# A two-layer decoder trunk: every compute engine in written order, one stream of weights, x transposed on the chip

## The chip, the core and the metric

The kernel runs on one core of a Trainium2 chip. Its engines are TensorE (PE: products and transposes), ScalarE (ACT), VectorE (DVE) and GpSimd (POOL); SyncE (SP) issues most transfers. Each engine works through its own list in order and waits at semaphores. The metric is the time of one execution in microseconds on the device.

## What is computed

Two pre-norm residual layers over 256 positions of width 1024, in float32. Layer 0 mixes with two parallel groups of eight heads: A, latent attention with low-rank q and kv and rotated parts, and B, dilated attention, written here as one table of biases. Layer 1 mixes with grouped-query attention over a window of 128 with a learned sink for each head. Each mixer is followed by a SwiGLU block of width 2816. From the reference, cut:

```python
h = x
for layer in range(DEPTH):                       # 2
    hn = _rmsnorm(h, attn_norm[layer])
    if layer % 2 == 0:
        mix = _even_mixer(hn, w_in, g_q, g_kv, w_uq, w_ukv, w_out, cos, sin, dil_slopes)
    else:
        mix = _odd_mixer(hn, w_qkv, sinks, w_out, swa_slopes)
    h = h + mix
    h = h + _swiglu(_rmsnorm(h, ffn_norm[layer]), w_gate_up[layer], w_down[layer])
return _rmsnorm(h, final_norm)
```

## The kernel before

**Products in three parts.** A float32 factor is split into hi, its value rounded to the engine's fp32r format, and lo, the rest. A product is then hi x hi, hi x lo and lo x hi, three matmuls into one PSUM tile (`mm3`, L116 to L126). A tile named `wh_x` is the hi copy of weight x, `wl_x` its rest, `raw_x` what arrived.

**Weights.** They arrive in units of up to 1 MB in a pool of three (`raw`), on SyncE's queue. Chunks of 128 x 512 are split: the hi copy on ScalarE (L93), the rest on VectorE or, for parts of b, wo0, qc and wo1, on GpSimd (`rest`, L73 to L78; L94). Seven pieces (two chunks each) fit in the pool of split weights. Names: c the joint low-rank projection, b the q, k, v of group B, uq and ukv the expansions of A, wo0 and wo1 the output projections, gu and dn the feed-forward blocks, kv and qc the projections of layer 1.

**The start.** x arrives twice: transposed (`xT`, eight row blocks, in five transfers), from which ScalarE and VectorE make the hi and lo parts with the gain (`xTh`, `xTl`), and plain (`h`), for norms and residuals. Then the products with c, the norms of c (`rstd_n`, `rstd_c`), the first products with b, transposes of c (`cT`), uq and ukv, and the rotation of q (`qA`).

**Attention.** Heads go in pairs: a0 to a3, b0 to b3 in layer 0, c0 to c7 in layer 1. A pair takes transposes of q and k (`T`), scores (`s`), on VectorE the minimum of the negated score with bias (`sn`, `nm`), on ScalarE the exponential with its sum (`e`, `sm`), the reciprocal (`rs`), on GpSimd the normalisation (L422), on TensorE the transposes of the weights (`pT`), their split into `pTh` (ScalarE) and `pTl` (VectorE), the values (`o`), and their split (`oT`). In layer 1 GpSimd writes the negated sink of each head into two columns of `sn` (L402). Iteration i runs the scores of pair i, the transposes of pair i + 1 and the values of pair i - 1, with other products between (`attention`, L479).

**Feed-forward.** For each of eleven groups of 256 columns: gate and up in one tile (`f0g`), Silu, product, transpose, and then the products with dn. The new h is formed in four quarters (`new_h`, L619): added (`h`), scaled by the gain (`hg`), transposed (`hT`) and split (`hTh`, `hTl`).

**Order.** TensorE's list is written by hand in the early part, the attentions and the end of each output projection; elsewhere, and on all other engines, a scheduler orders the work. Helpers hold several operations in one line, so rows name tiles.

## Time and profile before

| | |
|---|---|
| median of 3 runs | 590.8 us (589.92 to 591.53) |
| the profiled execution | 591.05 us |
| its span | 589.3 us |
| TensorE busy | 563.4 us, 96% |
| VectorE busy | 361.1 us, 61% |
| ScalarE busy | 335.9 us, 57% |
| GpSimd busy | 94.0 us, 16% |
| transferred | 101.57 MB, mean 172 GB/s |

A busy TensorE has matmuls in flight, each of which overlaps the next; the share says where none was in flight, not how fast they ran. Busy times of the other engines count their instructions alone.

### The profile page before, as it was taken

Reading aid. Unit: us, or ns where it says so; the run is one execution under the profiler, and the core shown is the slowest. Engines: PE = TensorE matmul, PEld = TensorE weight load, DVE = VectorE, ACT = ScalarE, POOL = GpSimd, SP = SyncE. Lnnn points to the kernel's source line nnn. Section 1 sums busy time; section 2 is a strip of 40 time slices with the busy share of each in tenths; the row PEclk is TensorE's granted clock in tenths of the full one; section 3 lists DMA queues with packets and bytes.
Section 4 is the critical chain, followed back from the end, with each engine's and each line's share of the span. In section 5 each row is a group of like instructions: output and inputs, shape, how many; then the busy total and the mean of one; then the engine's idle time right before and its main releaser. Section 6 shows DMA issues by size and latency. Waiting matters only on the chain.

```text
span 589.3 us, 7653 instructions
## 1 busy us (share of the span) xinstructions
PE 563.4 (96%) x2661; PEld 459.1 (78%) x2661; DVE 361.1 (61%) x742; ACT 335.9 (57%) x732; POOL 94.0 (16%) x157
## 2 busy tenths in 40 slices
PE   7798999899999999999999999999999999999995
PEld 5587787778888888888888777768888888888884
DVE  4578678786655565554559468777556556654524
ACT  5687788656545555544338787756555455454412
POOL 1169653110000000000001664300000000000000
PEclk9899999999999999999999999999999999999998
DMA  7777523336555555555546534226555565555301
GB/s 246 294 254 266 199 83 115 105 142 237 167 191 202 162 207 171 186 195 172 205 143 216 194 117 170 73 72 213 199 196 185 174 212 157 202 190 173 137 1 71
DMA packets 18183, 101.57 MB, mean 172 GB/s; under 512 B 2272, under 2 KB 3168, under 8 KB 7520
## 3 DMA queue, kind: packets, MB, share of 16 engines
q1 hardware_dynamic: 17712, 100.55, 49.5%
q10 hardware_dynamic: 432, 0.53, 0.2%
q8 instruction: 21, 0.34, 0.2%
q14 instruction: 18, 0.15, 0.1%
HBM read 100.02 MB, written 1.05 MB: 172 GB/s over the span
## 4 chain that ended last, share of the span: by engine, by line
PE 76%; ACT 8%; DVE 7%; DMA 3%; issue 2%; POOL 2%; SPq 0%; POOLq 0%; DVEq 0%; ACTq 0%
PE f0g L126 7%; PE f1g L126 7%; PE f1g L124 7%; PE f0g L124 7%; PE f1g L125 7%; PE f0g L125 7%; PE f0d L124 3%; PE f0d L125 3%; PE f0d L126 3%; PE f1d L124 3%; PE f1d L125 3%; PE f1d L126 3%; DMA h<-in_x_dram 2%; PE p L124 1%; DVE wl_gu L94 1%
## 5 line engine op out<-in xcount | busy, mean ns | idle before, releaser
L94 DVE TENSOR_TENSOR wl_gu<-raw_gu,wh_gu 128x512 fp32r<-128x512 f32 x176 | 116.4, 693 | 67.7 <-ACT wh_gu L93 66.1
L93 ACT CAST wh_gu<-raw_gu 128x512 fp32r<-128x512 f32 x176 | 102.2, 619 | 76.1 <-PE f0g L126 33.1
L94 DVE TENSOR_TENSOR wl_dn<-raw_dn,wh_dn 128x512 fp32r<-128x512 f32 x88 | 57.5, 689 | 54.8 <-ACT wh_dn L93 54.8
L93 ACT CAST wh_dn<-raw_dn 128x512 fp32r<-128x512 f32 x88 | 50.8, 619 | 61.6 <-PE f1d L126 23.3
L124 PE MATMUL f1g<-wh_gu,hTh_p 128*128 128x512 f32 x176 | 69.7, 396 | 0.0
L124 PE MATMUL f0g<-wh_gu,hTh_p 128*128 128x512 f32 x176 | 69.7, 396 | 0.0
L126 PE MATMUL f0g<-wh_gu,hTl_p 128*128 128x512 f32 x176 | 68.7, 390 | 0.7 <-DVE hTl_p L142 0.7
L126 PE MATMUL f1g<-wh_gu,hTl_p 128*128 128x512 f32 x176 | 68.7, 390 | 0.6 <-DVE hTl_p L142 0.6
L125 PE MATMUL f0g<-wl_gu,hTh_p 128*128 128x512 f32 x176 | 68.5, 389 | 0.0
L125 PE MATMUL f1g<-wl_gu,hTh_p 128*128 128x512 f32 x176 | 68.5, 389 | 0.0
L126 PEld LDWEIGHTS f0g<-wh_gu,hTl_p 128*128 128x128 f32 x176 | 33.0, 188 | 8.1 <-DVE hTl_p L142 1.1
L126 PEld LDWEIGHTS f1g<-wh_gu,hTl_p 128*128 128x128 f32 x176 | 33.0, 188 | 8.1 <-DVE hTl_p L142 1.1
L124 PEld LDWEIGHTS f0g<-wh_gu,hTh_p 128*128 128x128 f32 x176 | 33.1, 188 | 6.5 <-ACT hTh_p L141 0.2
L125 PEld LDWEIGHTS f0g<-wl_gu,hTh_p 128*128 128x128 f32 x176 | 33.1, 188 | 6.5
L125 PEld LDWEIGHTS f1g<-wl_gu,hTh_p 128*128 128x128 f32 x176 | 33.1, 188 | 6.4
L124 PEld LDWEIGHTS f1g<-wh_gu,hTh_p 128*128 128x128 f32 x176 | 33.1, 188 | 6.5
L124 PE MATMUL f0d<-wh_dn,f0fTh 128*128 128x512 f32 x88 | 34.5, 392 | 0.0
L124 PE MATMUL f1d<-wh_dn,f1fTh 128*128 128x512 f32 x88 | 34.3, 390 | 0.0
L126 PE MATMUL f0d<-wh_dn,f0fTl 128*128 128x512 f32 x88 | 34.3, 390 | 0.0
L126 PE MATMUL f1d<-wh_dn,f1fTl 128*128 128x512 f32 x88 | 34.2, 389 | 0.0
L125 PE MATMUL f1d<-wl_dn,f1fTh 128*128 128x512 f32 x88 | 34.2, 389 | 0.0
L125 PE MATMUL f0d<-wl_dn,f0fTh 128*128 128x512 f32 x88 | 34.2, 389 | 0.0
(299 smaller groups left out, 1134.9 us busy)
## 6 DMA issues: line engine op xcount, KB each, us to landing
raw_gu<-in_w_gu_dram SPq DMA_DIRECT2D x44, 1024.0 KB, 4.8
raw_dn<-in_w_dn_dram SPq DMA_DIRECT2D x22, 1024.0 KB, 4.8
raw_wo<-in_w_wo_dram SPq DMA_DIRECT2D x8, 1024.0 KB, 5.1
raw_b<-in_w_b_dram SPq DMA_DIRECT2D x4, 1024.0 KB, 5.1
raw_qc<-in_w_qc_dram SPq DMA_DIRECT2D x4, 1024.0 KB, 4.9
bias<-in_bias_dram SPq DMA_DIRECT2D x12, 256.0 KB, 3.9
raw_b<-in_w_b_dram SPq DMA_DIRECT2D x4, 512.0 KB, 10.0
gain<-in_gains_dram SPq DMA_DIRECT2D x4, 512.0 KB, 4.0
```

Of the source, the lines that this page charges most:

```text
L93: nc.scalar.copy(hi[:, a:e], part)
L94: rest(name, u).tensor_sub(lo[:, a:e], part, hi[:, a:e].bitcast(F32))
L124: nc.tensor.matmul(out, ah, wh, start=first, stop=False)
L125: nc.tensor.matmul(out, ah, wl, start=False, stop=False)
L126: nc.tensor.matmul(out, al, wh, start=False, stop=last)
```

## The change

The lists of TensorE, ScalarE, VectorE and GpSimd are now all as written in the program; SyncE's is still the scheduler's. The weights are one stream in a written order: c, two units of b, uq, ukv, the rest of b, wo0, gu0, dn0, kv, qc, wo1, gu1, dn1. A chunk is split after each 1024 columns of products (`settle`), up to eight chunks ahead of their use (`AHEAD`); a unit is loaded two units ahead. Outside the attentions ScalarE makes all hi copies and VectorE all rests. In the attentions ScalarE and VectorE take turns at the hi copies, GpSimd makes all rests, and the chunks are split at the end of an iteration. xT is not loaded any more: x arrives in eight pieces of 128 x 256, TensorE transposes it in sixteen transposes, and hi and lo are made from PSUM. Three products that only keep TensorE busy are added. The rotation of q is on VectorE for both halves (before: GpSimd for one). The squares of the feed-forward norms come after seven triples of products, Silu one triple later, the transposes of the new h 1500 columns after its sum (before 2000 or 2100). The attention is cut into pieces (minimum, exponential, normal, upper, lower) whose order is written.

```diff
--- before.py
+++ after.py
@@ -22,19 +22,8 @@
...
+    engines = mybir.EngineType
+    ctx.enter_context(
+        tc.manual_schedule(engines={engines.PE, engines.Activation, engines.DVE, engines.Pool}))
...
+    order = ["c", "b", "uq", "ukv", "b", "wo0", "gu0", "dn0", "kv", "qc", "wo1", "gu1", "dn1"]
+    early_b = 2
+    units = []
...
-    def rest(name, u):
-        if name not in POOLED or (name in ("b", "qc") and u < 3):
-            return nc.vector
-        pooled[0] += 1
-        return nc.vector if pooled[0] % 3 == 0 else nc.gpsimd
...
+    def emit_chunk():
+        i, name, p, base, a, e = chunks[state["emitted"]]
+        state["emitted"] += 1
+        while state["loaded"] <= min(i + 2, len(units) - 1):
+            load_next()
+        if (name, p) not in pieces:
...
+        if state["mode"] == "plain":
+            nc.scalar.copy(hi[:, a:e], part)
+            nc.vector.tensor_sub(lo[:, a:e], part, hi[:, a:e].bitcast(F32))
+        else:
+            state["turn"] += 1
+            if state["turn"] % 2:
                 nc.scalar.copy(hi[:, a:e], part)
-                rest(name, u).tensor_sub(lo[:, a:e], part, hi[:, a:e].bitcast(F32))
...
+            else:
+                nc.vector.tensor_copy(hi[:, a:e], part)
+            nc.gpsimd.tensor_sub(lo[:, a:e], part, hi[:, a:e].bitcast(F32))
...
+    AHEAD = 8
+    def pump(n):
+        for _ in range(n):
+            if state["emitted"] < len(chunks) and state["emitted"] - state["used"] < AHEAD:
+                emit_chunk()
...
+    def settle():
+        n = state["columns"] // 1024
+        state["columns"] -= 1024 * n
+        pump(n)
...
+        state["columns"] += out.shape[-1]
+        if state["auto"]:
+            settle()
+        for it in list(later):
...
+    def load_x(q):
+        for b in range(2):
+            nc.sync.dma_start(h[b][:, q * 256 : (q + 1) * 256], dr["x"][b * P : (b + 1) * P, q * 256 : (q + 1) * 256])
+    for q in range(3):
+        load_x(q)
+        load_next()
+    load_x(3)
...
+    state["auto"] = False
     for q in range(4):
-        xq = big.tile([P, 512], F32, tag="big", name=f"xT{q}")
+        pt = any_att(f"xT{q}")
+        for j in range(2):
+            for b in range(2):
+                nc.tensor.transpose(
+                    pt[:, (2 * j + b) * P : (2 * j + b + 1) * P],
+                    h[b][:, (2 * q + j) * P : (2 * q + j + 1) * P], ident)
         hi = tpool.tile([P, 512], F32R, tag="hTh", bufs=4, name=f"xTh{q}")
         lo = tpool.tile([P, 512], F32R, tag="hTl", bufs=4, name=f"xTl{q}")
...
                 hT[b][1][kt] = lo[:, j * S + b * P : j * S + (b + 1) * P]
+            emit_chunk()
         if q == 0:
-            load("c", 2, lambda: nc.sync.dma_start(xq[:, 0:256], dr["xT"][:, 0:256]))
-            nc.sync.dma_start(xq[:, 256:512], dr["xT"][:, 256:512])
-            part_weight("c", lambda: part_x(0))
+            keep_warm(3, False, True)
...
     mask = cpool.tile([P, S], F32, tag="mask", name="mask")
-    load("b")
-    load("uq")
-    load("ukv")
-    nc.sync.dma_start(rope, dr["rope"].rearrange("p (b t f) -> p b t f", b=2, t=3))
-    nc.sync.dma_start(mask, dr["mask"])
-    cT, kr, cgs = [], [], []
+    pump(2)
     ms0 = small.tile([P, 2], F32, tag="ss2", name="ss_n0")
-    for b in range(2):
-        mean_squares(h[b], 1.0 / 32.0, ms0[:, b : b + 1], f"n0{b}")
+    mean_squares(h[0], 1.0 / 32.0, ms0[:, 0:1], "n00")
+    pump(1)
+    mean_squares(h[1], 1.0 / 32.0, ms0[:, 1:2], "n01")
+    pump(1)
     rstd0 = rsqrt_eps(ms0, "n0")
...
+    def rotate(b, half):
+        r = qA[b][half]
+        x1, x2 = r[:, :, 64:80], r[:, :, 80:96]
+        cos, nsin, sin = (rope[:, b, i, :].rearrange("p (h f) -> p h f", f=16) for i in range(3))
+        tt = [work.tile([P, 4, 16], F32, tag="ropet", bufs=4, name=f"ropet{b}{half}{i}") for i in range(2)]
+        nc.vector.tensor_mul(tt[0], x2, nsin)
+        nc.vector.tensor_mul(tt[1], x1, sin)
+        nc.vector.tensor_mul(x1, x1, cos)
+        nc.vector.tensor_mul(x2, x2, cos)
+        nc.vector.tensor_add(x1, x1, tt[0])
+        nc.vector.tensor_add(x2, x2, tt[1])
+    for half in range(2):
+        for b in range(2):
...
-            eng = nc.gpsimd if half else nc.vector
...
+        def begin(self, i):
+            sn = work.tile([P, 386], F32, tag="sn", bufs=3, name=f"sn_{self.name}{i}")
+            nm = small.tile([P, 2], F32, tag="nm", name=f"nm_{self.name}{i}")
+            sm = small.tile([P, 2], F32, tag="sm", name=f"sm_{self.name}{i}")
+            if self.sinks[i] is not None:
+                nc.gpsimd.tensor_copy(sn[:, 128:130], self.sinks[i].to_broadcast([P, 2]))
+            self.st[i] = sn, nm, sm
         def scores(self):
...
+        def minimum(self, k):
+            b, i = self.order[k]
+            if self.st[i] is None:
+                self.begin(i)
+            sn, nm, sm = self.st[i]
             n, a, ba = ((128, 0, 128), (256, 130, 0))[b]
+            sink = self.sinks[i]
             nc.vector.tensor_tensor_reduce(
-                out=sn[:, a : a + n], in0=ps, in1=bias[:, ba:256], op0=ALU.add, op1=ALU.min,
+                out=sn[:, a : a + n], in0=self.ps[i][b], in1=self.bias(i)[:, ba:256], op0=ALU.add, op1=ALU.min,
...
+            if cur:
+                cur.minimum(0)
+            if done:
+                done.lower(1)
+            if cur:
+                cur.exp(0)
+                cur.minimum(1)
+                cur.exp(1)
+                cur.minimum(2)
+                cur.minimum(3)
+            other(i, 2 if many > 4 else 1)
+            rest = ahead[0]() if ahead else []
+            if last:
+                last.turn_p(0)
+            do(rest[:1])
+            other(i, 1)
+            rest2 = ahead[1]() if len(ahead) > 1 else []
+            if last:
+                last.turn_p(1)
+            do(rest[1:])
+            do(rest2)
+            if i + 1 < n:
+                pairs[i + 1].begin(0)
+            if cur:
+                cur.exp(2)
+                if not cur.split:
+                    cur.normal(0)
+                cur.exp(3)
+                if cur.split:
+                    cur.normal(0)
+                cur.normal(1)
+            other(i, many)
+            settle()
+            if last:
...
         gu = f"gu{layer}"
-        parts = {}
+        after(7 * 512, lambda: rs.extend(row_rstd(name)))
...
+            after(512, lambda ch=ch, pg=pg: gated(ch, pg))
```

The first place is SyncE's list in the start; raw_c is a unit of c, raw_b one of b, h the plain x. x2 marks two rows that read alike. Before:

```order
L65 DMA raw_c_2_135<-in_w_c_dram 128x832
L185 DMA xT2_132<-in_xT_dram 128x512
L65 DMA raw_c_3_151<-in_w_c_dram 128x832
L185 DMA xT3_148<-in_xT_dram 128x512
L196 DMA h0_214<-in_x_dram 128x1024
L196 DMA h1_215<-in_x_dram 128x1024
L65 DMA raw_b_0_218<-in_w_b_dram 128x1024 x2
L199 DMA gqkv_233<-in_gqkv_dram 128x384
L65 DMA raw_b_1_235<-in_w_b_dram 128x1024 x2
L65 DMA raw_b_2_252<-in_w_b_dram 128x2048
L65 DMA raw_uq_0_254<-in_w_uq_dram 128x1536
L65 DMA raw_ukv_0_256<-in_w_ukv_dram 128x1024
```

Now:

```order
L188 DMA h0_101<-in_x_dram 128x256
L188 DMA h1_102<-in_x_dram 128x256
L254 DMA gqkv_257<-in_gqkv_dram 128x384
L338 DMA rope_259<-in_rope_dram 128x384
L360 DMA mask_260<-in_mask_dram 128x256
L640 DMA bias0_926<-in_bias_dram 128x512
L640 DMA bias1_1037<-in_bias_dram 128x512
L640 DMA bias2_1132<-in_bias_dram 128x512
L702 DMA gain0_1418<-in_gains_dram 128x1024
L78 DMA raw_c_3_158<-in_w_c_dram 128x416 x2
L78 DMA raw_b_0_190<-in_w_b_dram 128x1024 x2
L78 DMA raw_b_1_222<-in_w_b_dram 128x1024 x2
```

The loads of rope, mask, bias and gain stood behind the units of b, and now stand ahead of the fourth unit of c.

The second place is GpSimd's list in attention 1, around pair c2; sn is the sink copy, e the normalisation, wl_wo1 the rests. Before:

```order
L94 TENSOR_TENSOR wl_wo1_1_1_3682<-raw_wo1_1_3673,wh_wo1_1_1_3681 128x512
L402 COPY sn_c21_3386<-nsink_2994 128x2
L422 TENSOR_SCALAR e_c10_3284<-e_c10_3284,rs_c10_3287 128x128
L422 TENSOR_SCALAR e_c10_3284<-e_c10_3284,rs_c10_3287 128x256
L402 COPY sn_c30_3467<-nsink_2994 128x2
L422 TENSOR_SCALAR e_c11_3290<-e_c11_3290,rs_c11_3293 128x128
L422 TENSOR_SCALAR e_c11_3290<-e_c11_3290,rs_c11_3293 128x256
L94 TENSOR_TENSOR wl_wo1_2_0_3850<-raw_wo1_2_3847,wh_wo1_2_0_3849 128x512
L94 TENSOR_TENSOR wl_wo1_2_1_3856<-raw_wo1_2_3847,wh_wo1_2_1_3855 128x512
L402 COPY sn_c31_3473<-nsink_2994 128x2
L422 TENSOR_SCALAR e_c20_3381<-e_c20_3381,rs_c20_3384 128x128
```

Now:

```order
L467 TENSOR_SCALAR e_c11_3330<-e_c11_3330,rs_c11_3372 128x128
L467 TENSOR_SCALAR e_c11_3330<-e_c11_3330,rs_c11_3372 128x256
L102 TENSOR_TENSOR wl_wo1_1_3383<-raw_wo1_0_3147,wh_wo1_1_3382 128x512 x2
L433 COPY sn_c21_3411<-nsink_3034 128x2
L433 COPY sn_c30_3453<-nsink_3034 128x2
L467 TENSOR_SCALAR e_c20_3409<-e_c20_3409,rs_c20_3459 128x128
L467 TENSOR_SCALAR e_c20_3409<-e_c20_3409,rs_c20_3459 128x256
L467 TENSOR_SCALAR e_c21_3416<-e_c21_3416,rs_c21_3463 128x128
L467 TENSOR_SCALAR e_c21_3416<-e_c21_3416,rs_c21_3463 128x256
L102 TENSOR_TENSOR wl_wo1_2_3478<-raw_wo1_1_3192,wh_wo1_2_3477 128x512 x2
```

The copy for c21 (second head of pair c2) stood ahead of the normalisations of pair c1 and stands now behind them and two rests of wo1.

The third place is VectorE's list where attention 0 ends and feed-forward 0 begins; h is the new sum, hg with its gain, hTl its rest. Before:

```order
L624 TENSOR_TENSOR hg_p010_1423<-h1_215,gain0_1380 128x512
L142 TENSOR_TENSOR hTl_p000_1434<-hT_p000_1428,hTh_p000_1433 128x512
L622 TENSOR_TENSOR h1_215<-p011_996,h1_215 128x512
L142 TENSOR_TENSOR hTl_p001_1480<-hT_p001_1474,hTh_p001_1479 128x512
L624 TENSOR_TENSOR hg_p011_1441<-h1_215,gain0_1380 128x512
L206 TENSOR_SCALAR ss_f01_1452<-ss_f01_1452 128x1
L94 TENSOR_TENSOR wl_gu0_2_1_1582<-raw_gu0_2_1573,wh_gu0_2_1_1581 128x512
L142 TENSOR_TENSOR hTl_p010_1492<-hT_p010_1486,hTh_p010_1491 128x512
L94 TENSOR_TENSOR wl_gu0_3_0_1623<-raw_gu0_3_1620,wh_gu0_3_0_1622 128x512
L142 TENSOR_TENSOR hTl_p011_1507<-hT_p011_1501,hTh_p011_1506 128x512
L94 TENSOR_TENSOR wl_gu0_3_0_1623<-raw_gu0_3_1620,wh_gu0_3_0_1622 128x512
L673 SCALAR_TENSOR_TENSOR f0f00_1565<-f0g00_1458,rstd_f00_1449,f0s00_1563 128x256
```

Now:

```order
L95 TENSOR_TENSOR wl_gu0_1_1453<-raw_gu0_0_1183,wh_gu0_1_1452 128x512
L708 TENSOR_TENSOR h1_102<-p010_1024,h1_102 128x512
L710 TENSOR_TENSOR hg_p010_1457<-h1_102,gain0_1418 128x512
L162 TENSOR_TENSOR hTl_p000_1468<-hT_p000_1462,hTh_p000_1467 128x512
L95 TENSOR_TENSOR wl_gu0_1_1453<-raw_gu0_0_1183,wh_gu0_1_1452 128x512
L162 TENSOR_TENSOR hTl_p001_1482<-hT_p001_1476,hTh_p001_1481 128x512
L708 TENSOR_TENSOR h1_102<-p011_1025,h1_102 128x512
L710 TENSOR_TENSOR hg_p011_1486<-h1_102,gain0_1418 128x512
L162 TENSOR_TENSOR hTl_p010_1501<-hT_p010_1495,hTh_p010_1500 128x512
L95 TENSOR_TENSOR wl_gu0_2_1510<-raw_gu0_1_1351,wh_gu0_2_1509 128x512
L162 TENSOR_TENSOR hTl_p011_1522<-hT_p011_1516,hTh_p011_1521 128x512
L95 TENSOR_TENSOR wl_gu0_2_1510<-raw_gu0_1_1351,wh_gu0_2_1509 128x512
```

A piece of gu0 is two chunks. Before, five pieces were split ahead of hTl_p000 and the sixth (wl_gu0_2_1: second of the third unit) stood beside it; now it is the second (wl_gu0_1), and the third stands behind the work on the last quarter of h.

## Rows read from the trace of the kernel before

**Rows 1.** The page, busy time, share of the span and instructions by engine.

```profile
PE 563.4 (96%) x2661; PEld 459.1 (78%) x2661; DVE 361.1 (61%) x742; ACT 335.9 (57%) x732; POOL 94.0 (16%) x157
```

**Rows 2.** Stretches: length, busy PE, PEld, DVE, ACT, POOL (x instructions), clock, DMA.

```profile
0.00:32.30 32.30, 24.50 (x98) 18.10 (x99) 15.10 (x35) 17.74 (x40) 4.33 (x13) 0.95 0.78 269
...
50.50:118.20 67.70, 63.62 (x339) 51.24 (x338) 48.57 (x147) 51.47 (x146) 32.80 (x47) 1.00 0.43 148
...
134.00:312.00 178.00, 178.00 (x813) 147.46 (x812) 102.72 (x168) 88.52 (x165) 2.13 (x4) 1.00 0.54 184
312.00:333.70 21.70, 20.46 (x119) 17.21 (x118) 14.12 (x24) 16.60 (x36) 8.40 (x7) 1.00 0.68 232
333.70:389.50 55.80, 52.87 (x276) 41.78 (x275) 40.79 (x130) 42.30 (x124) 25.71 (x53) 1.00 0.38 132
...
405.00:570.00 165.00, 165.00 (x751) 136.71 (x750) 92.57 (x151) 81.51 (x151) 0.00 (x0) 1.00 0.50 173
```

**Rows 3.** What TensorE waited for: total us, times, longest.

```profile
PE c L124 <- ACT xTh L170: 3.5, 3, 1.8
PE b L124 <- ACT wh_b L93: 3.1, 1, 3.1
PE o_c L443 <- DVE pTl_c L142: 2.6, 6, 0.8
PE T_a L460 <- ACT qk_a L532: 2.2, 4, 0.8
PE o_b L443 <- DVE pTl_b L142: 2.1, 3, 1.2
...
PE b L124 <- DVE vAl L142: 0.9, 1, 0.9
```

**Rows 4.** Two stretches of the start, columns as in rows 2.

```profile
17.50:20.00 2.50, 0.90 (x5) 0.54 (x3) 0.17 (x1) 1.26 (x4) 0.69 (x1) 1.00 1.04 416
...
22.50:25.00 2.50, 2.50 (x7) 1.93 (x7) 1.71 (x4) 2.47 (x8) 0.43 (x1) 0.52 0.31 128
```

**Rows 5.** Timeline of the start: start, length, and idle before with its releaser.

```profile
13.20 0.98 ACT L93 CAST wh_c<-raw_c 128x416 fp32r<-128x416 f32 x2 [2.05 <-DMA raw_c<-in_w_c_dram]
...
20.81 1.13 ACT L93 CAST wh_b<-raw_b 128x512 fp32r<-128x512 f32 x2
...
21.47 0.79 PE L124 MATMUL b<-wh_b,xTh 128*128 128x512 f32 x1 [3.07 <-ACT wh_b L93]
```

**Rows 6.** Timeline of TensorE at the end of attention 0.

```profile
122.94 0.66 PE L629 MATMUL hT_p<-ident,hg_p 128*128 128x128 f32 x4
```

**Rows 7.** Instructions on tile qA, duration ns min/median/max, first and last start.

```profile
L338 DVE TENSOR_TENSOR ropet<-qA,rope x2: 213/287/361, 37.2 to 40.2; 128x64 f32<-128x64 f32 x2
```

**Rows 8.** The same for tile wl_b, weight rests of b on both engines.

```profile
L94 DVE TENSOR_TENSOR wl_b<-raw_b,wh_b x16: 682/748/1598, 21.5 to 52.6; 128x512 fp32r<-128x512 f32 x16
L94 POOL TENSOR_TENSOR wl_b<-raw_b,wh_b x8: 1294/1722/1742, 43.1 to 53.6; 128x512 fp32r<-128x512 f32 x8
```

**Rows 9.** Timeline of one iteration of attention 1.

```profile
353.08 0.33 DVE L409 CUSTOM_DVE_ANT_0 sn_c<-s_c,bias,nsink 128x128 f32<-128x128 f32 x1
...
353.84 0.40 ACT L414 ACTIVATE e_c<-sn_c,nm_c 128x129 f32<-128x129 f32 x1
...
354.35 0.38 ACT L141 CAST qT_c<-T_c 128x256 fp32r<-128x256 f32 x1
...
354.62 0.52 ACT L414 ACTIVATE e_c<-sn_c,nm_c 128x257 f32<-128x257 f32 x1
...
355.13 0.47 ACT L141 CAST pTh_c<-pT_c 128x384 fp32r<-128x384 f32 x1
...
355.36 0.19 POOL L402 COPY sn_c<-nsink 128x2 f32<-128x2 f32 x1 [1.75 <-ACT e_c L414]
...
355.49 0.52 ACT L414 ACTIVATE e_c<-sn_c,nm_c 128x257 f32<-128x257 f32 x1
355.53 0.83 POOL L422 TENSOR_SCALAR e_c<-e_c,rs_c 128x128 f32<-128x128 f32 x2
```

More of the change, by code (lines that the diff above doesn't have):

```diff
@@ new lines, in trunk @@
+    early_b = 2
+    units = []
+    for at, name in enumerate(order):
+        n_units = dr[name][0].shape[0]
+        first, last = (0, early_b) if at == 1 else (early_b, n_units) if at == 4 else (0, n_units)
+        units += [(name, u) for u in range(first, last)]
+    chunks = []
+    for i, (name, u) in enumerate(units):
+        src, n, kts = dr[name]
+        per = n * kts
+        step = 512 if per in (512, 1024) else 416 if per == 832 else 384
+        count = src.shape[2] // per
+        for p in range(count):
+            for a in range(0, per, step):
+                chunks.append((i, name, u * count + p, p * per, a, min(per, a + step)))
@@ L99, in fetch @@
-    def fetch(name, parts=1):
-        load(name, parts)
-        part_weight(name)
-    def piece(name, i):
-        while name not in streams or len(streams[name]["pieces"]) <= i:
-            if name not in streams or not streams[name]["raw"]:
-                load(name)
-            part_weight(name)
-        return streams[name]["pieces"][i]
+        for j in range(parts):
+            nc.sync.dma_start(raw[:, j * cut : (j + 1) * cut], src[u][:, j * cut : (j + 1) * cut])
+        raws[i] = raw
@@ new lines, in trunk, with at @@
+    AHEAD = 8
[3 more added lines that the diff above has]
+                emit_chunk()
+    def at(name, p, kt, a, b):
+        while (name, p) not in pieces or [c for c in chunks[state["emitted"] :] if c[1:3] == (name, p)]:
+            emit_chunk()
+        n = dr[name][1]
+        hi, lo = pieces[name, p]
+        step = next(c[5] - c[4] for c in chunks if c[1:3] == (name, p))
+        state["used"] += (b - a) / (2.0 * step)
+        return hi[:, kt * n + a : kt * n + b], lo[:, kt * n + a : kt * n + b]
@@ L424, in normal @@
                 )
-            return e
         def turn_p(self, i):
@@ L477, in pair_scores, with attention @@
         return run
[L479 removed]
+    def attention(pairs, between, fill):
         n = len(pairs)
+        state["auto"], state["mode"] = False, "beside"
+        oT[:] = pairs
         def other(i, k):
[L485 to L486 removed]
+            do(fill[i][:k])
             del fill[i][:k]
[L489 to L512 removed]
```

443 lines of the change are left out of this document (204 added, 239 removed).

## Prediction

> **What bounds the kernel now.** I read the page first: TensorE is busy in 563.4 of 589.3 us [rows 1], so the kernel can only win or lose the 26 us of the span in which TensorE stands still, plus what it does slowly, and any new standstill adds in full. The profiled execution took 591.05 us, 0.25 above the median of the runs, 590.8; differences below are put on the median.
>
> Next the busy time by stage says where those 26 us lie [rows 2]. In both feed-forward blocks TensorE is busy in 178.00 of 178.00 and 165.00 of 165.00 us: nothing is to be had there, unless the weights come late. The standstill is 7.8 us in the start (0 to 32.3), 4.1 in attention 0, 1.2 in the projections of layer 1 and 2.9 in attention 1; most of the rest is the entry into attention 0 and the tail, of which the change leaves the tail alone.
>
> Then what ended the standstill [rows 3]: at the start the parts of x on ScalarE (3.5 us) and the first hi copy of b (3.1); in the attentions the rests and copies that VectorE and ScalarE make late (o_c 2.6, T_a 2.2, o_b 2.1). After the 3.07 us before b, TensorE also ran at a granted clock of 0.52 from 22.5 to 25 [rows 4], so that wait cost some 1.7 us more than its length.
>
> Last, the limits outside TensorE. From 17.5 to 20 us the DMA engines moved 416 GB/s at full share [rows 4]: the start is limited by arrival. ScalarE got the fourth c unit at 13.20 and first b unit at 20.81 [rows 5].
>
> **The start.** Removed: the 1.05 MB of xT. Added: x in eight pieces ahead of c's third and fourth unit, sixteen transposes (four of h take 0.66 us now [rows 6], so 2.6 us together) that lie inside the 7.8 us of standstill, and three more warming products, likewise covered. Moved, by SyncE's order: gqkv, rope, mask, three biases and a gain now stand ahead of the fourth c unit. By their shapes that is 0.20 + 0.20 + 0.13 + 0.79 + 0.52 = 1.84 MB. Ahead of that unit then stand 1.05 (x) + 1.84 - 0.79 (the xT that stood there) = 2.1 MB more than before. At 416 GB/s this is 5.0 us, less about 1 because before the queue moved less than that while it waited for slots: the unit lands near 17.3, not 13.2. Its splitting takes 0.8 us, c's last twelve products 2.2 at full clock and 4.4 at half; c ends at 20.3 to 22.5. The first half of b is 0.52 MB behind, at 18.6, and ScalarE's written order takes it at once, where before it stood behind the squares until 20.81: b no longer waits. So b begins about when it did (21.47 [rows 5]). Against that, VectorE's order puts the rests of b's second unit behind the whole norm chain (two powers on GpSimd, four squares on ScalarE, four scalings): TensorE waits 1.7 to 3 us in the middle of b. It saves the half-clock stretch only if c ends without a long wait, which the 4 us before the fourth c unit make unlikely. I take 0, between -4 (the loads in front move aside, no clock loss) and +4 (clock loss and the full wait for b).
>
> **Entry into attention 0.** All 24 rotations are on VectorE: 12 x 0.287 us = 3.4 us more than before if each lasts as now [rows 7]. Most of this runs while TensorE has products to do; I count 0.7 us for the two weight rests that now queue behind rotations, against the 0.9 us that a b product now waits for vAl behind VectorE's queue [rows 3]: -0.2. If all of it shows, +3.3.
>
> **Attention 0.** The late rests o_b and T_a (4.3 us together) come partly from weight rests queued on VectorE, which last 748 ns in the middle and up to 1598 [rows 8]. With all rests on GpSimd these queue no longer; I count 3.4 of the 4.3 as gone. Against it GpSimd's order puts the second rest of b's eighth piece behind four normalisations at the first iteration: 1.9 us of wait. Sum -1.5, between -4 (no such wait) and +2 (rests at 1722 ns each [rows 8] on GpSimd).
>
> **Feed-forward.** Same products, same split by ScalarE and VectorE, with a lead of four to five chunks by the new rule (one for every 1024 columns, 1.4 us of products, against 0.68 us of VectorE for a rest [rows 8]): 0. The deferred Silu and squares are covered by 102 us of VectorE work in 178 [rows 2].
>
> **Attention to feed-forward, twice.** VectorE's order there: the add, the gain and the rest of the last quarter of h now stand ahead of the rests of the third gate-up piece, while before five pieces had been split by then. Each operation of this shape takes 0.68 us alone [rows 8]; the two chunks come 0.35 and 0.55 late: +0.9 each, +1.8 (0 to +3).
>
> **Projections of layer 1.** The 1.2 us of standstill go if the moved copies come in time; one product triple more (0.7 us) is done before the attention: -0.6.
>
> **Attention 1.** This is the largest term. GpSimd's order in every iteration is: sink copy of the pair's second head, four normalisations, two weight rests, then the sink copy of the next pair's second head. The minimum and the exponential of that head wait for that copy, so the iteration closes a loop on GpSimd. Its length from the rows [rows 9]: copy 0.19; minimum 0.33 with 0.06 before and 0.09 behind it; then ScalarE in its written order, by the starts of these operations now: exponential 0.51, first half of pTh 0.36, qT 0.27, second half of pTh 0.36; from the start of the long exponential to that of the first normalisation 0.91; two pairs of normalisations 2 x 0.83; two rests 2 x 1.29 [rows 8]. Sum 7.32, with the steps between the last ones 7.4 us. Before, the copies stood a pair earlier and part of the rests on VectorE, and eight pairs took 55.8 us from first score to last values [rows 2]. Now: 8.2 us from the first score until the first copy in the loop (0.5 scores, 0.5 minimum, exponentials, qT, reciprocal, normalisations to 5.6, two rests), six rounds of 7.4, 1.3 for the one iteration that has three rests, and from the last copy 4.75 to the last normalisation and 2.4 for transposes, split and values: 8.2 + 44.4 + 1.3 + 7.2 = 61.1. That is +5.3. If only the exponential waits for the copy the round is 6.95 and the term +2.5; if the rests last 1722 ns each it is +10.
>
> What speaks for still more: VectorE makes every second hi copy beside GpSimd. VectorE's rests, 0.68 us alone, last up to 1.60 when GpSimd makes rests too, and GpSimd's 1.29 become 1.74 [rows 8]. The Trainium skill, "SBUF — State Buffer", section "Who interferes with whom", says that a VectorE copy can take the port pair that it shares with GpSimd, and that the second to start blocks fully; the trace agrees that the two hold each other up with rests, and has no such copy. By that rule a copy would hold GpSimd up by its own length once in a round, an estimate of up to 0.69 us or +4 in all; by the shortest row of GpSimd's rests (1.29) the term stays 5.3.
>
> **Sum.** 0 - 0.2 - 1.5 + 0 + 1.8 - 0.6 + 5.3 = +4.8: 595.6 us.
>
> **Rivals.** (a) GpSimd does not close the loop, because the exponential overlaps or the rests of one iteration run under the next's scores. Point of decision: a round of attention 1 under 6.6 us, TensorE's own 52.87 / 8 [rows 2]. Then the written order only removes waits there: of the 2.9 us idle some 2 go, the term is -2.0 and the sum -2.5: 588.3 us, faster. For it: GpSimd was busy in only 25.71 of 55.8 us [rows 2]; against: the order of its rows. (b) The start gains: the loads in front move in parallel or the clock stays up, b begins 5 us earlier: 4.8 - 5 = -0.2, 590.6, no change. For it: 1.05 MB less before b's products; against: 1.84 MB ahead. (c) Both: 583.3. (d) GpSimd is blocked by VectorE's copies in each round: +9 to +10, 600. For it: the 1598 and 1742 ns rows; against: the 1294 of the same row, which stands where VectorE did other work.
>
> **Numbers.** Forecast (593 to 599) 0.45, (a) 0.17, (b) 0.18, (c) 0.10, (d) 0.10. A measurement of this kernel tells 0.3%, 1.8 us, from no change. Faster: (a), (c) and a little of (b), 0.30; same: 0.15; slower: 0.55. Range 585.5 to 601: it leaves out (c) and the far end of (d).
>
> **What would show it.** Right: sink copies on GpSimd starting straight after two rests, rounds of 7.4 us between first scores, TensorE waiting for o_c or pT by GpSimd; a wait in b for wl_b of the second unit; the fourth c unit taken near 17 us. Wrong: rounds under 6.6; b's first product before 18 us; any standstill inside the feed-forward blocks, which would mean that the lead of the split is too short, and would cost most.

## The result, and the profile after

The changed kernel takes 614.09 us (median of 4 runs, 612.73 to 615.71) against 590.85 in the same session: a ratio of 1.0395 (1.0359 to 1.0432), slower by 23.2 us. The sign of the forecast was right; its size was not, and the time lies 13 us above the upper end of the range. The profiled execution took 615.37 us with a span of 613.6, so 24.3 us more span than before.

First the head of the page after, the counterpart of [rows 1]: busy time, share of the span and instructions of each engine.

```profile
PE 574.2 (94%) x2680; PEld 465.8 (76%) x2680; DVE 349.9 (57%) x760; ACT 320.5 (52%) x709; POOL 102.2 (17%) x157
```

TensorE stands still for 613.6 - 574.2 = 39.4 us instead of 25.9, so 13.5 of the 24.3 are new standstill. The other 10.8 are busy time, though it has only 19 instructions more (sixteen transposes, three warming products): it must also have run slower somewhere.

To place both, the next table cuts the two traces at the same events (first or last matmul on a named tile). It is worked out from the starts and lengths of TensorE's rows. f0d and f1d are the products with dn; in names of tiles below, `_p` is the new h behind an output projection and `_f` the one behind a feed-forward block.

| stage, from and to | before | after | difference | forecast |
|---|---|---|---|---|
| start, to the end of cT | 32.34 | 35.69 | +3.35 | 0 |
| entry, to the first score | 18.19 | 18.17 | 0.0 | -0.2 |
| attention 0, to the last o_b | 67.62 | 76.27 | +8.65 | -1.5 |
| end of wo0, to the first f0g | 6.49 | 7.02 | +0.5 | with f0g, f1g: +1.8 |
| f0g | 126.49 | 128.60 | +2.1 | |
| f0d | 61.25 | 63.30 | +2.05 | 0 |
| projections of layer 1, to the first score | 21.29 | 21.62 | +0.3 | -0.6 |
| attention 1, to the last o_c | 55.81 | 61.91 | +6.1 | +5.3 |
| end of wo1, to the first f1g | 6.42 | 6.24 | -0.2 | |
| f1g | 126.47 | 127.80 | +1.3 | |
| f1d | 60.31 | 60.33 | 0.0 | 0 |

Stretches of the trace after, cut at three of these stages (columns as in [rows 2]): the start and the two attentions.

```profile
0.00:35.69 35.69, 28.25 (x117) 21.90 (x118) 16.95 (x38) 18.14 (x42) 8.62 (x25) 0.90 0.71 245
...
53.86:130.13 76.27, 66.87 (x338) 52.98 (x337) 39.71 (x142) 44.25 (x130) 46.16 (x57) 0.96 0.28 95
...
350.67:412.58 61.91, 54.08 (x271) 42.12 (x270) 33.75 (x126) 37.14 (x114) 39.93 (x67) 0.97 0.29 98
```

In attention 0 TensorE stood still for 76.27 - 66.87 = 9.4 us, where [rows 2] shows 4.1. Busy time rose as well, 66.87 against 63.62 for about as many instructions, at a mean granted clock of 0.96. In the start the standstill is no larger than before (7.4 against 7.8); it is the busy time that grew.

What TensorE waited for after, the counterpart of [rows 3]: total us, times, longest.

```profile
PE o_c L486 <- DVE pTl_c L162: 4.3, 5, 2.2
PE pT_c L476 <- DVE nm_c L446: 3.4, 5, 1.0
PE T_a L509 <- ACT qk_a L616: 2.7, 3, 1.2
PE c L136 <- ACT wh_c L94: 2.6, 1, 2.6
PE pT_b L476 <- DVE nm_b L446: 2.5, 3, 1.1
PE b L136 <- ACT wh_b L94: 2.0, 1, 2.0
PE b L137 <- DVE wl_b L95: 1.7, 3, 0.8
PE hT_f L715 <- DVE hg_f L710: 1.7, 3, 0.6
PE b L137 <- POOL wl_b L102: 1.7, 1, 1.7
PE f0g L138 <- DVE hTl_p L162: 1.4, 1, 1.4
PE f1g L138 <- DVE hTl_p L162: 1.4, 1, 1.4
...
PE b L136 <- ACT wh_b L99: 1.0, 1, 1.0
```

The old waits for xTh, o_b and vAl are gone; T_a is not, it stands at 2.7 us after 2.2. New are waits for weights split too late (c, b), for the minima of the scores (`pT` behind `nm`) and for the new h (`hT_f`; `hTl_p` doubled). The wait for `o_c`, behind the GpSimd chain in attention 1, grew from 2.6 to 4.3.

**The start.** Timeline after of SP's issues, ScalarE and TensorE, each row from its engine's list.

```profile
9.19 1.38 SPq L640 DMA_DIRECT2D bias<-in_bias_dram  x3
...
11.16 1.01 SPq L78 DMA_DIRECT2D raw_c<-in_w_c_dram  x2
...
17.49 0.54 ACT L94 CAST wh_c<-raw_c 128x416 fp32r<-128x416 f32 x1 [3.78 <-DMA raw_c<-in_w_c_dram]
...
18.08 0.64 PE L136 MATMUL c<-wh_c,xTh 128*128 128x416 f32 x1 [2.64 <-ACT wh_c L94]
...
22.19 0.39 PE L136 MATMUL b<-wh_b,xTh 128*128 128x512 f32 x1
...
29.78 0.50 PE L136 MATMUL b<-wh_b,xTh 128*128 128x512 f32 x1 [1.99 <-ACT wh_b L94]
```

The three biases are issued ahead of the fourth c unit, ScalarE takes that unit at 17.49 and b begins at 22.19: the forecast said 17.3, and about 21.5. The wait in the middle of b is there too.

**Attention 0, its first iterations**, from the lists of GpSimd, ScalarE, VectorE and TensorE after.

```profile
59.41 0.83 POOL L467 TENSOR_SCALAR e_a<-e_a,rs_a 128x128 f32<-128x128 f32 x2 [2.80 <-DVE rs_a L465]
...
60.43 0.61 ACT L99 CAST wh_b<-raw_b 128x512 fp32r<-128x512 f32 x1
60.64 0.74 DVE L101 CAST wh_b<-raw_b 128x512 fp32r<-128x512 f32 x2
60.82 1.18 POOL L467 TENSOR_SCALAR e_a<-e_a,rs_a 128x128 f32<-128x128 f32 x2 [0.58 <-DVE rs_a L465]
61.09 0.49 PE L136 MATMUL b<-wh_b,xTh 128*128 128x512 f32 x1 [0.98 <-ACT wh_b L99]
61.97 2.49 POOL L102 TENSOR_TENSOR wl_b<-raw_b,wh_b 128x512 fp32r<-128x512 f32 x2
63.28 0.80 PE L137 MATMUL b<-wl_b,xTh 128*128 128x512 f32 x1 [1.69 <-POOL wl_b L102]
```

The product at 61.09 needs a chunk whose hi copy ScalarE began only at 60.43, and the one at 63.28 a rest that GpSimd began at 61.97, behind four normalisations. No split chunk was left: these products wait for their own split, at the end of an iteration.

The granted clock on both sides of these two waits, from windows of after.

```profile
60.00:62.00 2.00, 0.60 (x2) 0.19 (x1) 0.82 (x3) 1.04 (x4) 1.42 (x4) 1.00 0.00 0
62.00:69.50 7.50, 6.22 (x17) 4.97 (x18) 1.29 (x8) 2.18 (x6) 4.97 (x4) 0.54 0.41 140
69.50:90.00 20.50, 18.01 (x103) 14.80 (x102) 9.07 (x35) 11.21 (x33) 10.23 (x14) 1.00 0.16 52
```

After the waits of 0.98 and 1.69 us TensorE ran for seven microseconds at the lower level, 0.5: this is part of the extra busy time. Other such stretches lie, in windows of 1 us, at 18 to 22, 32 to 35 and 363 to 367, each behind a standstill; before, [rows 4] show the only one of the start.

**Attention 1, one round**, lists of GpSimd, ScalarE, VectorE and TensorE after, to be read beside [rows 9].

```profile
385.69 1.80 POOL L467 TENSOR_SCALAR e_c<-e_c,rs_c 128x128 f32<-128x128 f32 x4 [2.55 <-DVE rs_c L465]
387.46 2.52 POOL L102 TENSOR_TENSOR wl_wo<-raw_wo,wh_wo 128x512 fp32r<-128x512 f32 x2
389.93 0.30 POOL L433 COPY sn_c<-nsink 128x2 f32<-128x2 f32 x2
...
388.80 0.35 DVE L446 CUSTOM_DVE_ANT_0 sn_c<-s_c,bias,nsink 128x128 f32<-128x128 f32 x1
...
390.14 0.41 ACT L458 ACTIVATE e_c<-sn_c,nm_c 128x129 f32<-128x129 f32 x1 [1.22 <-POOL sn_c L433]
...
389.31 0.52 PE L476 MATMUL pT_c<-ident,e_c 128*128 128x128 f32 x3 [0.53 <-DVE nm_c L446]
...
392.58 0.72 PE L486 MATMUL o_c<-pTh_c,vC 128*128 128x512 f32 x2 [0.34 <-DVE pTl_c L162]
```

GpSimd makes four normalisations, two rests, then the copy, and ScalarE's exponential waits 1.22 us for that copy. The loop is the one that was forecast. The minimum at 388.80 did not wait for it, so the shorter of the two forecast rounds applies: 6.95 was said, 7.08 to 7.10 us lie between the first scores of the last three rounds. The four normalisations took 1.80 us, where the forecast had 2 x 0.83: 0.14 more, as much as the round has over 6.95.

### The profile page after: what moved, and what is told of

The parts are those of the page before. It is cut to its first block, busy times and chain, and to the rows that moved or that the text cites. A ratio compares the mean times of both kernels' runs of the same rounds, so it can differ in the third digit from the quotient of the medians.

```text
span 613.6 us, 7647 instructions
## 1 busy us (share of the span) xinstructions
PE 574.2 (94%) x2680; PEld 465.8 (76%) x2680; DVE 349.9 (57%) x760; ACT 320.5 (52%) x709; POOL 102.2 (17%) x157
## 4 chain that ended last, share of the span: by engine, by line
PE 73%; DVE 10%; ACT 6%; POOL 5%; issue 3%; DMA 3%; SPq 1%; POOLq 0%; DVEq 0%; ACTq 0%
PE f1g L138 6%; PE f1g L136 6%; PE f1g L137 6%; PE f0g L137 6%; PE f0g L138 6%; PE f0g L136 6%; PE f1d L138 3%; PE f1d L137 3%; PE f1d L136 3%; PE f0d L136 3%; PE f0d L137 3%; PE f0d L138 3%; POOL wl_wo L102 2%; PE b L137 2%; PE b L138 1%
## 5 line engine op out<-in xcount | busy, mean ns | idle before, releaser
L95 DVE TENSOR_TENSOR wl_gu<-raw_gu,wh_gu 128x512 fp32r<-128x512 f32 x173 | 109.2, 691 | 1.3 <-ACT wh_gu L94 0.8
L94 ACT CAST wh_gu<-raw_gu 128x512 fp32r<-128x512 f32 x173 | 94.7, 620 | 0.1
L95 DVE TENSOR_TENSOR wl_dn<-raw_dn,wh_dn 128x512 fp32r<-128x512 f32 x88 | 55.7, 688 | 29.2 <-ACT wh_dn L94 29.1
L94 ACT CAST wh_dn<-raw_dn 128x512 fp32r<-128x512 f32 x88 | 48.9, 621 | 34.2 <-PE f1d L138 15.8
L102 POOL TENSOR_TENSOR wl_wo<-raw_wo,wh_wo 128x512 fp32r<-128x512 f32 x32 | 40.6, 1288 | 1.8 <-ACT wh_wo L99 1.4
L237 POOL TENSOR_TENSOR rstd_n<-ss_n,mhalf 128x2 f32<-128x2 f32 x2 | 1.4, 712 | 209.5 <-DVE ss_n L236 209.5
```

The source lines that it names most:

```text
L94: nc.scalar.copy(hi[:, a:e], part)
L95: nc.vector.tensor_sub(lo[:, a:e], part, hi[:, a:e].bitcast(F32))
L102: nc.gpsimd.tensor_sub(lo[:, a:e], part, hi[:, a:e].bitcast(F32))
L237: nc.gpsimd.tensor_tensor(out=r, in0=ms, in1=mhalf[:, :w], op=ALU.pow)
```

## Experiments

The theory after this reading: four separate places lose the time, and each can be mended alone. (1) The written stream brings no lead of split weights into attention 0. (2) VectorE's order puts the minima behind the rests of the values. (3) The constants stand ahead of c's fourth unit. (4) The sink copy closes a loop on GpSimd. Beside these, (5) the transposes 1500 columns after the sum of h come too soon. The rivals: GpSimd has too many rests in the attentions, wherever they stand; and the start loses by the clock alone. All kernels below are the changed kernel with the edit shown, numbered in this order. The ratio behind each time is to the kernel before, with its 95% interval.

**1. One chunk more for every 1024 columns, outside the attentions.**

```diff
         state["columns"] -= 1024 * n
-        pump(n)
+        pump(n + 1 if n and state["auto"] else n)
```

> The changed kernel took 614.1 us. This one splits one chunk more at each step outside the attentions, so that the lead really grows to eight. Theory 1 (the lead of the split weights has shrunk to nothing where attention 0 begins, TensorE waits there for pieces split on demand, and its clock falls to half): the waits for wh_b and wl_b in attention 0 (1.0 and 1.7 us) and the 6 us at a clock of 0.5 behind them (3 us lost) go, the first two rounds of attention 0 shrink from 10.4 and 11.9 us to about 8.5 each: 607 to 609. Rival (GpSimd's rests of 1.29 us each are too slow, whenever they are asked for): the waits only move to a later round, gain under 2 us: 612 to 614.

Measured: 609.55 us, 1.0311 (1.028 to 1.0342). Attention 0 took 69.53 us, its first two rounds 6.77 and 9.49 instead of 10.44 and 11.93, and the waits of b in it are gone. In the first round that is the gain of the lead, in the second the clock: the seventh kernel, with the same late splits and a clock of 1.00 there, shows 9.97 and 9.52. f0g fell to 127.90. The wait T_a grew to 4.9 us, all of the growth ahead of attention 0, whose entry took 18.93 us instead of 18.17: a part of what was won is held up by the next edge.

**2. The minima ahead of the two rests of the values.**

```diff
                 done.upper(1)
-                done.lower(0)
             if cur:
                 cur.minimum(0)
-            if done:
-                done.lower(1)
-            if cur:
                 cur.exp(0)
...
                 cur.minimum(3)
+            if done:
+                done.lower(0)
+                done.lower(1)
```

> Only VectorE's order is changed in both attentions: the four minima of a pair stand ahead of the two rests of the values of the pair before the last. Theory 2 (TensorE waits for pT because a PSUM bank is freed by a minimum that is written behind a rest, and that rest waits for ScalarE): the waits for pT (2.5 in layer 0, 0.5, 3.4 in layer 1) go: 608 to 610. Rival (the rounds are set by GpSimd's loop of sink copy, normalisations and two rests, 7.1 us, and in attention 0 by late weights): PE waits elsewhere for the same time, 612.5 to 614.

Measured: 609.45 us, 1.0328 (1.028 to 1.0377). All waits of pT are gone, attention 0 took 70.55 us. In attention 1 the last rounds stayed near 7.1 and the wait for o_c grew from 4.3 to 7.8 us: there the GpSimd loop sets the pace, and the time only moved from one wait to the other.

**3. The constants on ScalarE's queue**, in ScalarE's written order, so that SP's list holds only x and weights in the start.

```diff
-    nc.sync.dma_start(gqkv, dr["gqkv"])
+    nc.scalar.dma_start(gqkv, dr["gqkv"])
...
-            nc.sync.dma_start(t, dr["bias"][i // 2].rearrange("p (h f) -> p h f", f=256))
+            nc.scalar.dma_start(t, dr["bias"][i // 2].rearrange("p (h f) -> p h f", f=256))
```

(rope, mask and the first gain likewise, the gain ahead of the attention.)

> Only the loads of gqkv, rope, mask, biases and the first gain are moved from SyncE's list to ScalarE's, where they stand in written order. Theory 3 (1.84 MB of them ahead of the fourth c unit are the loss of the start): the fourth c unit is taken near 14 us and not at 17.5, TensorE's wait of 2.64 us and the half clock behind it (1.9 us lost) go, cT ends near 32.0 and not at 35.7: 610 to 611. Rival (the small pieces of x and c fill the queue, the constants only take room that stands empty): the unit is taken at 16 or later, gain under 1 us.

Measured: 610.49 us, 1.0327 (1.0292 to 1.0362). b began at 17.60, cT ended at 30.02, 5.7 us earlier in the profiled runs; of this 3.6 us show in the medians. Against the 33.5 to 34.4 at which cT ends in other kernels that leave the start as it is, it is 3.5 to 4.3. A wait of 2.66 us for the second b unit is left, behind the norm chain.

**4. Both sink copies of the next pair ahead of the normalisations.**

```diff
                 pairs[i + 1].begin(0)
+                if pairs[i + 1].sinks[1] is not None:
+                    pairs[i + 1].begin(1)
```

> Only the sink copy of a pair's second head is moved: it stands beside that of the first head, ahead of the normalisations of the pair before. Forecast's own theory (GpSimd's closed loop sets the rounds of attention 1): rounds fall from 7.1 to between 6.3 and 6.6 us in the last four, attention 1 from 61.9 to 57 to 59: 609 to 611. Rival (the order of VectorE and ScalarE sets them too: the wait for pT stays): rounds stay above 6.9, gain under 1.5 us.

Measured: 605.63 us, 1.0249 (1.0214 to 1.0284). Timeline of this kernel in attention 1, rows of GpSimd and of ScalarE.

```profile
381.76 0.19 POOL L433 COPY sn_c<-nsink 128x2 f32<-128x2 f32 x1 [1.89 <-ACT e_c L458]
382.00 1.80 POOL L467 TENSOR_SCALAR e_c<-e_c,rs_c 128x128 f32<-128x128 f32 x4
383.77 2.53 POOL L102 TENSOR_TENSOR wl_wo<-raw_wo,wh_wo 128x512 fp32r<-128x512 f32 x2
...
385.54 0.41 ACT L458 ACTIVATE e_c<-sn_c,nm_c 128x129 f32<-128x129 f32 x1 [0.33 <-DVE nm_c L446]
```

The copy now stands ahead of the four normalisations and the two rests, and the exponential waits for a minimum, not for GpSimd. Rounds of 6.54 us, attention 1 in 54.74 us, 7.2 less (6.3 less than the 61.00 of the seventh kernel, whose clock stayed at 1.00 there), with the same rests on GpSimd. It was a place in a list, not a load.

**5. Every second rest in the attentions on VectorE** (the rival that GpSimd has too much).

```diff
-            nc.gpsimd.tensor_sub(lo[:, a:e], part, hi[:, a:e].bitcast(F32))
+            (nc.gpsimd if state["turn"] % 2 else nc.vector).tensor_sub(
+                lo[:, a:e], part, hi[:, a:e].bitcast(F32))
```

> Only this is undone: in the attentions every second rest (that of the chunks whose hi copy VectorE makes) is VectorE's again, not GpSimd's. Theory (GpSimd's list is what the rounds of attention 1 wait for): one rest less in a round, 1.29 us, takes the last rounds from 7.1 to what the other orders allow, 6.5, and attention 1 from 61.9 to 57 to 59: 609 to 611. Rival (a rest on VectorE, 0.69 us and more beside GpSimd, holds minima and pTl up by as much as it frees): gain under 1 us, or a loss.

Measured: 614.39 us, 1.0408 (1.0374 to 1.0443): no gain. Attention 1 fell to 56.82 us with rounds of 6.52, since one rest less stands in the loop. Attention 0 rose to 83.95 in the profiled execution, at a mean clock of 0.90:

```profile
52.50:136.45 83.95, 70.84 (x338) 56.25 (x337) 50.39 (x155) 44.12 (x130) 35.69 (x45) 0.90 0.26 87
```

About half of the rise is clock. The standstill is 13.1 us instead of 9.4: wl_b 2.9 instead of 1.7, pT_a 2.7 instead of 0.5 behind minima (pT_b is 2.4 and was 2.5). What VectorE takes over is late there, and the rival falls for attention 0.

**6. Thirteen warming products ahead of c's last twelve** (the rival that the start loses by the clock).

```diff
             c_products(q - 1)
+    keep_warm(13, True, True, acc("fill"))
     c_products(3)
```

> Thirteen products that only keep TensorE busy are put ahead of the products with the fourth c unit, where TensorE stands still for 2.6 us. Theory (the standstill costs its length and, by the half clock behind it, 1.9 us more): the clock stays at 1.0 from 15 to 22 us, b begins 1.5 to 2 us earlier (20.3 instead of 22.2): 612 to 612.5. Rival (what is behind waits for the arrival of b and the norm chain anyway): b's first product earlier, but cT ends within 0.5 us of now: 613.5 to 614.5.

Measured: 613.34 us, 1.0392 (1.0368 to 1.0416), within the run-to-run spread of the changed kernel. Windows of this kernel in the start:

```profile
15.00:18.00 3.00, 2.93 (x15) 1.38 (x14) 0.00 (x0) 0.52 (x2) 0.00 (x0) 1.00 1.02 384
...
26.00:30.00 4.00, 0.75 (x4) 0.33 (x2) 1.91 (x7) 1.40 (x4) 2.35 (x9) 0.94 0.27 99
30.00:33.00 3.00, 2.98 (x7) 1.99 (x8) 3.00 (x6) 2.07 (x5) 2.95 (x5) 0.51 0.01 3
```

The clock stayed at 1.00 through c and b began 1.3 us earlier, at 20.89. TensorE then stood still for 3.25 of the 4 us from 26 to 30, behind the norm chain, and ran at half clock after that. cT ended at 35.10, 0.6 us earlier: the next wait took most of the gain back.

**7. Longer distances for the transposes of the new h.**

```diff
-                new_h(b, self.po[b][n], n, g, self.name, 1500)
+                new_h(b, self.po[b][n], n, g, self.name, 2000)
...
-    ffn(0, lambda b, n, po: new_h(b, po, n, g1, "f0", 1500), "f0")
+    ffn(0, lambda b, n, po: new_h(b, po, n, g1, "f0", 2100), "f0")
```

> Only the distance of the transposes of the new h is put back from 1500 columns of products to 2000 (output projection) and 2100 (feed-forward 0). Theory (TensorE reaches these transposes before VectorE has formed hg): the three waits for hg_f (1.7 us) at the end of feed-forward 0 and those for hg_p (1.0) go, the stretch of the dn products shrinks from 63.3 to 61.5: 611.5 to 612.5. Rival (hTl or the kv products then wait instead): within 0.7 us of 614.1.

Measured: 615.02 us (610.03 to 618.94), 1.0416 (1.035 to 1.0483): no gain that can be told. In its trace f0d fell to 61.28 us as expected, but f0g rose to 131.02, with a wait of 2.4 us for hTl_p instead of 1.4, a new one of 0.7 for hTh_p, and a clock of 0.50 from 135 to 138. Behind the second output projection, where the clock stayed up, the end of wo1 and f1g took 0.7 us more together. So 2100 is right behind the feed-forward block, and 1500 behind an output projection. This trace is useful for a second reason. Attention 0 is unchanged in it, and its window reads:

```profile
51.66:125.05 73.39, 64.01 (x338) 50.86 (x337) 39.69 (x142) 44.13 (x130) 46.20 (x57) 1.00 0.29 100
```

The same 338 instructions stood still for 9.38 us, as in after (9.40), but the granted clock stayed at 1.00 and busy time was 2.86 us less. So of the +8.65 of attention 0, 5.8 remain at full clock, 5.3 of them standstill (9.4 against 4.1), and 2.9 are the clock of that one execution.

**8. All five together** (the first four edits and this one).

> The edits of the first four experiments and of the last one together. If the parts are separate the gains add: 4.5 (lead), 4.6 (minima first), 3.6 (constants), 8.5 (sink copies), 1.8 (distance): 591. If two of them cure the same wait (half-clock stretches in attention 0 by the lead and by the minima), 593 to 597. Rival (what remains is the written order as such): above 600.

Measured: 592.88 us (10 runs), 1.0043 (1.0021 to 1.0065). Attention 0 65.89 us, attention 1 51.04 with rounds of 5.9, cT at 32.55. The windows of the two attentions:

```profile
49.99:115.89 65.90, 62.67 (x338) 51.07 (x337) 38.44 (x142) 42.77 (x129) 44.08 (x56) 1.00 0.33 109
336.20:387.24 51.04, 50.80 (x271) 40.62 (x270) 34.32 (x127) 36.74 (x113) 40.76 (x67) 1.00 0.42 137
```

Left are T_a 4.0, the second b unit 3.3 and hTl_p 2.4 and 1.6. The single gains of the first four, 4.5, 4.6, 3.6 and 8.5, sum to 21.2, as much as the four with the distance gave together. That they match so closely is in part chance, as a single gain holds clock too. In attention 1 the minima, worth nothing alone, took 3.7 us more off the 54.74 once the copies were moved.

**9. The same, with 1500 again behind the output projections, and b's second unit split ahead of the norms of c.**

```diff
             mean_squares(pc[b][:, a:e], 1.0 / math.sqrt(e - a), ms[:, i : i + 1], f"c{b}{j}")
+    pump(2)
...
+    pump(2)
     r = rsqrt_eps(ms, "c")
```

> As the kernel with all edits (592.9), with two differences. The distance of 2000 columns is taken only at the end of feed-forward 0 (2100), the output projections keep 1500: there 2000 made the wait for hTl longer (2.4 us and 3.4 us of half clock behind it), so the gate-up stretches should fall from 130.5 and 129.7 to about 128 each, 4 us together. And the second unit of b is split ahead of the norm chain, so that ScalarE's krn and VectorE's scalings no longer stand ahead of it: the wait of 3.3 us in b and the half clock behind it go, cT ends near 28.5 instead of 32.5. Theory: 584.5 to 587.5, faster than the kernel before. Rival (the norm chain is only moved: it holds cT or the entry into attention 0 up by as much): 588.5 to 591.

Measured: 585.65 us (585.27 to 586.77), 0.9917 (0.99 to 0.9934): 0.8% faster than before. cT ended at 27.54 with a clock of 1.00 throughout, f0g took 127.86 and f1g 127.83.

**10. In group A also the copies of q and k ahead of the split of pT.** The same instructions in another order in ScalarE's and VectorE's lists.

```diff
+            if cur and not cur.split:
+                do(rest[:1])
             if last:
                 last.turn_p(0)
-            do(rest[:1])
+            if not (cur and not cur.split):
+                do(rest[:1])
```

> As the one before it, and in the pairs of group A the copies of the first transposes of q and k stand ahead of the split of pT on ScalarE and VectorE. Theory (the second transposes wait for these copies, 4.0 us in four waits): 2 to 3 us of them go, 1.5 to 2.5 us faster than the one before. Rival (pTh and pTl are then later and the values wait): within 0.7 us of it.

Measured: 583.65 us (583.13 to 584.04), 0.988 (0.9865 to 0.9894), the fastest of all. The head of the list of waits of this kernel:

```profile
PE T_a L511 <- ACT qk_a L622: 1.9, 2, 1.7
PE f0g L138 <- DVE hTl_p L162: 1.4, 1, 1.4
PE f1g L138 <- DVE hTl_p L162: 1.4, 1, 1.4
```

T_a fell from 4.4 (in the ninth) to 1.9 us and attention 0 from 65.89 to 63.29. These waits end with a copy on ScalarE, and its place in the written lists is what cured them.

**11. The ninth kernel, with the longer lead growing inside the attentions too** (`n + 1 if n else n` in the first edit). The expectation calls the ninth, of 585.65 us, the tenth.

> As the tenth kernel, and the lead grows by one chunk a step in the attentions too. Theory (what is missing at the start of the feed-forward blocks is lead): the late rests of gu there vanish, 1 to 2 us faster than the tenth. Rival (the waits there are for hTl, and one more rest of 1.29 us on GpSimd in a round lengthens the rounds): equal or 1 to 4 us slower.

Measured: 584.53 us (583.66 to 585.52), 0.9901 (0.9882 to 0.9919): about 1.1 less than without, 0.7 of it before f0g (6.66 instead of 7.34); the intervals of the two overlap, so the sign is likely and no more.

**12. The early split of b's second unit alone**, on the changed kernel.

> The changed kernel (614.1) with one edit: the second unit of b is split ahead of the norm chain of c. Theory (written order puts these chunks behind krn and the scalings, TensorE waits 2.3 us in the middle of b and then runs 3.5 us at half clock): b runs without a wait, cT ends at 30 to 31.5 instead of 34 to 35.7, and since the edit adds four chunks to the lead, the wait for wl_b in attention 0 (1.7) goes too: 606 to 609. Rival (cT waits for the norm chain instead): the stretch to cT stays within 1 us: 611.5 to 613.5 from the lead alone.

Measured: 604.97 us (604.53 to 605.18), 1.024 (1.0225 to 1.0255), 9.1 us less by one edit that moves four chunks, more than expected. cT ended at 32.76, not at 30 to 31.5, and attention 0 took 69.52 us: the same as the first experiment's 69.53, which gave the lead in another way. No product of b waited for its split any more. The four chunks serve twice, in b's own middle and as the lead with which attention 0 begins. Not all of the 9.1 is order: attention 0 is 6.8 us shorter than in the trace of the changed kernel, and 2.9 of these are the half clock that this trace doesn't have there.

## Why the prediction was right in sign and wrong in size

**The step that failed: "With all rests on GpSimd these queue no longer; I count 3.4 of the 4.3 as gone", the -1.5 of attention 0.** It measured +8.65 in the profiled execution and +5.8 where the clock stayed up, 10.2 of the 19.5 us by which the trace exceeds the forecast +4.8. Of the two waits counted as gone only o_b (2.1) went. T_a grew from 2.2 to 2.7, in attention 0 itself from 1.4: it waits for ScalarE's copies of q and k, and the tenth kernel cures it by their place in the lists alone, with the rests where they were. The step also priced what the rests do to VectorE's queue and did not count how many chunks are split when the attention begins. The one wait it did name, the rest behind four normalisations at 1.9 us, came at 1.69; but it came with a late hi copy (0.98) ahead of it, and behind it a slow stretch. From the 73.4 us at full clock, more lead alone gives 69.5 (-3.9), minima first alone gives 70.6 (-2.8), and the two with the other edits 65.9. So the two causes account for the rise almost additively. That 65.9 lies 1.7 below before, near the -1.5, is chance: the 1.9 us that the -1.5 holds as a loss are mended in it, and of the 3.4 only half shows.

**A cause not in the forecast at all** is the second of these. I had the pieces of the attention in the diff, and read GpSimd's list around them but not VectorE's, where a minimum (which frees the scores' bank for pT) stands behind rests that wait for ScalarE.

**Attention 1: mechanism right, size by luck.** +6.1 against +5.3, by the loop on GpSimd that the forecast spelled out, shown by moving one copy. Errors cancel in the size: only the exponential waits, so by the forecast's own working the term should have been +2.5, 8.2 + 43.0 + 7.2 us. Between GpSimd's copies the trace has 8.6 + 44.9 + 8.5. The six rounds in the middle hold 0.14 us each for slower normalisations and about 0.9 for a stretch at half clock (44.0 in the third kernel, without it); the last pair took 1.3 longer than was said. The point of decision in rival (a), 6.6 us as TensorE's own, was too high: rounds of 5.9 occur in the eighth kernel. Its whole attention 1, 51.04 us, is shorter than the 52.87 us of busy time from which the point was taken; a busy time is not a floor.

**The start: both details right, the sum of 0 too low.** +3.35 lies inside the -4 to +4 that was said, near its bad end: the fourth c unit at 17.49, the wait behind the norm chain 1.99 + 0.32. The forecast's own terms, b no earlier and 1.7 to 3 us of wait in it, add up to +1.7 to +3; the 0 follows from none of them. The old standstill went, but new waits of the same length took its place, so the sixteen transposes (2.6 us by [rows 6], 2.9 in the trace, which I had hidden in it) and a second stretch at half clock come on top. Over kernels that leave the start as it is (the second, fourth, fifth and seventh here) cT ended between 33.5 and 34.4, so this profile is at the slow end.

**The entry** came out at 0.0 for -0.2; all rotations on VectorE cost nothing.

**Attention to feed-forward: right in kind, +1.8 forecast.** With the end of wo and f0g, f1g together 3.8. The wait for hTl_p is 1.4 us twice, after 0.7 and 0.6; f0g also lost 0.7 to the short lead (127.90 with more, though the stretch ahead of it then took 0.3 longer). A term was missing: the transposes at 1500 columns cost 1.7 us of waits for hg_f at the end of f0d, which had been put at 0. With 2100 it is 61.28, as before.

**The rivals.** None occurred as it was said. (a) to (c) needed an open loop or a faster start. (d), GpSimd held up by VectorE's copies by up to 0.69 us in a round, showed at a quarter of that. The 32 rests of wo took 1.29 us on average, the low end of [rows 8], but the hi copies meet the normalisations: after, the 20 of 128x256 with no hi copy beside them took 0.48 us, the 12 with one or two 0.64 to 0.91.

```profile
385.81 0.53 DVE L101 CAST wh_wo<-raw_wo 128x512 fp32r<-128x512 f32 x1
386.04 0.65 POOL L467 TENSOR_SCALAR e_c<-e_c,rs_c 128x256 f32<-128x256 f32 x1
```

That is 0.17 us a round here. The Trainium skill, "SBUF — State Buffer", section "Who interferes with whom", says that a VectorE copy in a mode that uses two ports and a GpSimd instruction shut each other out, and that the second to start blocks fully. The trace agrees that one holds the other up, by less than the copy's recorded length; whether the normalisation stood still for that time or ran slower, no row tells.

What stays open: which part of the 614 belongs to the clock in each single execution. The seventh kernel's four runs follow their mean granted clock (610.03 at 0.992, 612.89 at 0.983, 617.16 at 0.979, 618.94 at 0.977), but only the first was profiled, so where the others slowed isn't known.

## What to carry to other kernels

When a scheduler's order is replaced by a written one, follow each engine's list through one iteration and ask of every entry what it would wait for and who waits behind it; here one copy, two rests ahead of the minima, and four chunks to split, each at the wrong place, gave 4.6 to 9.1 us when they were moved. No engine had too much work: the fastest kernel has the instructions of the changed one in another order (one rest has gone from GpSimd to VectorE, and the constants are issued from ScalarE) and takes 30 us less. A stream of split weights needs its lead counted at the entry of each stage that cannot refill it: chunks split minus chunks used, in hand, at that point. Here none was left when attention 0 began, and the first round took 3.2 us longer for it. And when several such waits stand in one chain, mending one often only feeds the next (the warming products, the minima in attention 1), so an experiment with all of them together is worth as much as each alone.
